# Sliding 8x8 windows of a 16x64x64x64 tensor: how the input loads are divided between the queues

## The chip, the cores and the metric

One core of one Trainium2 chip. The metric is the device time of one execution in microseconds (us); the program is a pure copy, so DMA and the copies inside the core's memory are all its work.

## The reference

```python
batch, c, h, w = (16, 64, 64, 64)      # x, float32; window_size 8, stride 4
n_h = (h - window_size) // stride + 1  # 15
n_w = (w - window_size) // stride + 1  # 15
for i in range(n_h):
    for j in range(n_w):
        result[:, i, j] = x[:, :, i*4 : i*4 + 8, j*4 : j*4 + 8]
```

The output has the shape (16, 15, 15, 64, 8, 8): 16.78 MB go in, 58.98 MB come out. Every input element is written up to four times.

## The kernel before

**Layout.** The whole input is held in the on-chip tile Lt (L is its view). A partition holds 32 channels of 16 rows of one image: the partition number is half * 64 + y * 32 + (image within y) * 4 + q. The half ch is the lower (0, channels 0 to 31, partitions 0 to 63) or the upper one (partitions 64 to 127), y one of two groups of eight images, q the quarter of the image's height. One channel of one partition is 16 rows x 64 columns, 4,096 bytes that lie together in memory.

**Loads.** Two kinds. The first FC = 8 channels of each half are *staged*: eight transfers (one for each q and half) bring them for all 16 images into the buffer GG, which the output does not need yet, at partitions 32 to 95. ScalarE issues the four of the lower half, SyncE the four of the upper one (L124). The other 24 channels go straight to Lt, by `load` (L61), which for a given half, y and q writes eight partitions, every fourth one. There are eight pairs (y, q), in order. For each of the first six (HWP = 6), SyncE loads channels 12 to 31 of the lower half (20 channels, 640 KB), GpSimd channels 8 to 11 of the lower half (SMALL = 4, 128 KB), and then channels 8 to 31 of the upper half (24 channels, 768 KB). For the last two pairs GpSimd loads 24 channels of both halves and SyncE nothing. So SyncE has 4 staging transfers and 6 loads, GpSimd 16 loads. Transfers of a kind share eight semaphores in turn: each one's issue waits until the one eight places before it has landed.

**Moves.** 16 copies (L141), two channels of 32 partitions each, take the staged channels from GG to Lt, y = 0 before y = 1. Every third is ScalarE's, the others VectorE's: six and ten.

**Output.** ScalarE and VectorE copy windows from Lt into tiles cut from GG (`part`, L192; `plain`, L212 and L150; `cross`, L225, L150 and L229; the last line, L256), and GpSimd writes each tile out by an indirect scatter (L158): one row of the tile for each partition, 16,384 bytes in `part` (index idx_y), 24,576 in the others (idx, idx_lo, idx_hi). A row whose index is made too large by FAR is dropped. In `cross`, every partition with q = 3 of one half is dropped: idx_lo drops those of partitions 0 to 63, idx_hi those of 64 to 127. There are six `part` tiles, five `plain` and ten `cross` ones, and two last tiles that SyncE stores (L257). The scatters come in this order: part, part, part, plain, part, plain, part, plain, part, plain, then cross tiles, lo and hi in turn, with one more plain in the middle. From the fourth tile on three buffers rotate, so a tile's copies wait until the scatter three tiles back has left its buffer. `part` tiles of y = 0 need only the loads of the first four pairs; `plain` tiles need all. All scatters stand in GpSimd's DMA queue behind its loads.

Of the kernel before, what the change touches and what calls it, by code (L numbers as in the profile page):

```python
# [10 lines left out]
def kernel(  # L11
# [7 lines left out]
    nc = tc.nc  # L19
    P = nc.NUM_PARTITIONS  # L20

    B, C, H, W = x.shape
# [8 lines left out]
    CH = 2  # L31
    HQ = P // (B * CH)
    CL = C // CH
    RB = H // HQ
# [5 lines left out]
    NY = B // YB  # L40
# [11 lines left out]
    L = Lt[:, :, 0 : RB * W].rearrange("p c (r w) -> p c r w", r=RB)  # L52
# [1 line left out]

    SMALL, HWP = 4, 6

    def load(eng, ch, y, q, c0, c1):
        p0 = ch * HP + y * QP + q  # L60
        eng.dma_start(out=L[p0 : p0 + QP - HQ + 1 : HQ, c0:c1, :, :], in_=x_v[ch, y, q, :, c0:c1, :])  # L61
# [11 lines left out]
    LF = 3 * CFREE // 2  # L73
# [38 lines left out]

    NG = 3
    TC = CFREE // (RB * W)
    FC = 8
    CP = RB * W + PAD
    GG = gpool.tile([P, NG * LF], f32)
    assert CH * FC * CP <= NG * LF
    S = [GG[:, ch * FC * CP : (ch + 1) * FC * CP].rearrange("p (c f) -> p c f", c=FC)[:, :, 0 : RB * W].rearrange("p c (r w) -> p c r w", r=RB) for ch in range(CH)]
    x_b = x.rearrange("b (ch cl) (hq r) w -> ch hq b cl (r w)", ch=CH, hq=HQ)  # L120
    for q in range(HQ):
        for ch in range(CH):
            s = S[ch][QP + q : QP + q + (B - 1) * HQ + 1 : HQ]
            (nc.scalar, nc.sync)[ch].dma_start(out=s, in_=x_b[ch, q, :, 0:FC, :])  # L124

    for y in range(NY):
        for q in range(HQ):
            hw = y * HQ + q < HWP
            if hw:
                load(nc.sync, 0, y, q, FC + SMALL, CL)  # L130
            load(nc.gpsimd, 0, y, q, FC, FC + SMALL if hw else CL)
            load(nc.gpsimd, 1, y, q, FC, CL)

    PC = TC // 2
    first = [(0, ch, c) for ch in range(CH) for c in range(0, FC, PC)]
    then = [(1, ch, c) for ch in range(CH) for c in range(0, FC, PC)]
    for n, (y, ch, c) in enumerate(first + then):
        f = slice(QP + y * QP, QP + (y + 1) * QP)
        d = slice(ch * HP + y * QP, ch * HP + (y + 1) * QP)
        copy = nc.vector.tensor_copy if n % 3 else nc.scalar.copy  # L140
        tc.keep_in_program_order(copy(out=L[d, c : c + PC, :, :], in_=S[ch][f, c : c + PC]))  # L141

    o_v = out.rearrange("b i j c r w -> (b i j) (c r w)")
    o_l = out.rearrange("b i j c r w -> (b i j c r w)").rearrange("(n f) -> n f", f=LF)
# [103 lines left out]
    for s in range(2):  # L248
        t = tile_()
        g = halves(t, 3)  # L250
        for n, ch, cols in line(NR - 1):
            for y in range(NY):
                d = slice(QP + y * QP, QP + (y + 1) * QP)
                f = slice(ch * HP + y * QP, ch * HP + (y + 1) * QP)
# [38 lines left out]
```

## Time and profile before

| | us |
|---|---|
| median of 3 runs (185.74 to 185.79) | 185.74 |
| the profiled execution | 185.73 |
| its span in the profile | 184.0 |
| VectorE busy | 142.8 |
| ScalarE busy | 141.6 |
| GpSimd busy | 39.5 |

The span is the time from the first to the last instruction of the profiled execution; 1.73 us of its time lie around it. Matrix work there is none. In the slices of the profile each digit is the busy share of one fortieth of the span, 4.6 us, in tenths; the DMA row is the mean over 16 DMA engines, and GB/s is what they moved. DMA queue q0 is GpSimd's, q1 SyncE's, q10 ScalarE's, q14 fetches instructions. "SPq" and "ACTq" rows are work of an engine's sequencer, such as issuing a transfer. In a timeline, the first number is the start and the second the time until the group's end, with the wait before it in brackets.

### The profile page before, as it was taken

How to read it: one execution, taken by the hardware profiler on the slowest of the kernel's cores; microseconds unless marked ns; L12 is line 12 of the kernel's file. 1: busy time of each engine (PE TensorE's matmuls, PEld its weight loads, DVE VectorE, ACT ScalarE, POOL GpSimd, SP SyncE). 2: the span in 40 equal slices, each digit the busy share in tenths (PEclk: the TensorE clock that was granted, in tenths of full speed). 3: DMA queues.
4: the chain of work that ended last, by engine and by line, in shares of the span. 5: the costliest groups of instructions: out<-in, count | busy, mean ns of one | idle time of the engine just before them, and what ended most of it. 6: DMA issues, size and time to landing. Idle time of an engine off the chain costs nothing.

```text
span 184.0 us, 501 instructions
## 1 busy us (share of the span) xinstructions
DVE 142.8 (78%) x183; ACT 141.6 (77%) x82; POOL 39.5 (21%) x42
## 2 busy tenths in 40 slices
DVE  4002999999999949979999599898798869978700
ACT  0002999999999969989899489889787869978700
POOL 7500763033330420230122202211220220220000
DMA  4999999999999999999999999999999999999993
GB/s 150 400 412 409 411 413 410 399 394 443 422 431 440 433 431 447 413 435 444 419 438 438 433 429 433 444 433 428 428 428 433 428 435 433 428 428 428 428 428 134
DMA packets 9828, 75.80 MB, mean 412 GB/s; under 512 B 3072, under 2 KB 3072, under 8 KB 7168
## 3 DMA queue, kind: packets, MB, share of 16 engines
q0 software_dynamic: 7504, 64.50, 83.2%
q1 hardware_dynamic: 1744, 9.18, 12.2%
q10 hardware_dynamic: 576, 2.10, 3.1%
q14 instruction: 4, 0.03, 0.0%
HBM read 16.78 MB, written 62.91 MB: 433 GB/s over the span
## 4 chain that ended last, share of the span: by engine, by line
DMA 68%; DVE 19%; issue 3%; POOL 2%; ACT 2%; ACTq 0%; DVEq 0%; PEldq 0%
DMA out_dram<-GG,idx_lo 26%; DMA out_dram<-GG,idx 21%; DMA Lt<-in_x_dram 14%; DVE GG L192 8%; DMA out_dram<-GG,idx_hi 8%; DVE GG L150 7%; POOL Lt L61 2%; ACT GG L256 2%; DVE GG L229 2%; DVE GG L212 1%; ACTq L288 0%; DVE GG L256 0%; DVEq L150 0%; POOL pi L77 0%; DVEq L212 0%
## 5 line engine op out<-in xcount | busy, mean ns | idle before, releaser
L225 ACT COPY GG<-Lt 64x2048 f32<-64x2048 f32 x30 | 56.9, 1897 | 9.6 <-DMA out_dram<-GG,idx 4.8
L150 DVE STREAM_SHUFFLE GG<-Lt 64x1024 f32<-64x1024 f32 (+1 forms) x35 | 50.6, 1444 | 0.9
L192 DVE COPY GG<-Lt 32x2048 f32<-32x2048 f32 x30 | 36.6, 1219 | 4.4 <-DMA out_dram<-GG,idx 3.4
L192 ACT COPY GG<-Lt 32x2048 f32<-32x2048 f32 x18 | 34.1, 1896 | 2.8 <-DMA out_dram<-GG,idx 2.4
L212 ACT COPY GG<-Lt 64x2048 f32<-64x2048 f32 x15 | 28.3, 1897 | 0.8 <-DMA out_dram<-GG,idx_lo 0.5
L141 DVE COPY Lt<-GG 32x2048 f32<-32x2048 f32 x10 | 11.9, 1236 | 13.8 <-DMA GG<-in_x_dram 13.7
L229 DVE COPY GG<-Lt 64x1024 f32<-64x1024 f32 x30 | 20.5, 683 | 0.6
L61 POOL DMA_DIRECT2D Lt<-in_x_dram x16 | 13.8, 873 | 17.5 <-DMA Lt<-in_x_dram 16.8
L158 POOL DMA_INDIRECT out_dram<-GG,idx_y x6 | 9.5, 1578 | 30.7 <-DVE GG L192 26.3
L141 ACT ACT_TABLE_LOAD x1 | 1.3, 1283 | 17.1 <-DMA GG<-in_x_dram 17.1
L212 DVE COPY GG<-Lt 64x2048 f32<-64x2048 f32 x10 | 12.1, 1221 | 0.3
L256 ACT COPY GG<-Lt 32x768 f32<-32x768 f32 x12 | 10.0, 830 | 1.8 <-DMA out_dram<-GG,idx_hi 1.2
L158 POOL DMA_INDIRECT out_dram<-GG,idx_lo x5 | 4.8, 963 | 30.1 <-DVE GG L229 30.1
L141 ACT COPY Lt<-GG 32x2048 f32<-32x2048 f32 x6 | 11.2, 1894 | 0.1
L256 DVE COPY GG<-Lt 32x1280 f32<-32x1280 f32 x12 | 9.8, 819 | 1.6 <-DMA out_dram<-GG,idx_hi 0.9
L158 POOL DMA_INDIRECT out_dram<-GG,idx x5 | 6.2, 1246 | 19.8 <-ACT GG L212 16.7
L158 POOL DMA_INDIRECT out_dram<-GG,idx_hi x5 | 4.9, 976 | 26.0 <-DVE GG L229 18.0
L150 DVE LOAD_MASK_SELECT GG<-Lt x35 | 0.3, 8 | 8.2 <-DMA out_dram<-GG,idx 3.7
L80 DVE TENSOR_SCALAR tb<-pi 128x1 int32<-128x1 int32 x1 | 0.2, 155 | 1.0 <-POOL pi L77 1.0
L83 DVE TENSOR_SCALAR tb<-tb 128x1 int32<-128x1 int32 x2 | 0.3, 153 | 0.0
L86 DVE TENSOR_TENSOR th<-tc,tq 128x1 int32<-128x1 int32 x2 | 0.3, 152 | 0.0
L77 POOL IOTA pi<- 128x1 int32 x1 | 0.1, 124 | 0.4 <-PEq L288 0.4
(20 smaller groups left out, 2.9 us busy)
## 6 DMA issues: line engine op xcount, KB each, us to landing
Lt<-in_x_dram POOLq DMA_DIRECT2D x10, 768.0 KB, 17.8
Lt<-in_x_dram SPq DMA_DIRECT2D x6, 640.0 KB
out_dram<-GG SPq DMA_DIRECT2D x2, 1536.0 KB, 10.1
GG<-in_x_dram ACTq DMA_DIRECT2D x4, 512.0 KB, 14.3
GG<-in_x_dram SPq DMA_DIRECT2D x4, 512.0 KB, 14.7
Lt<-in_x_dram POOLq DMA_DIRECT2D x6, 128.0 KB, 17.8
out_dram<-GG,idx_y POOLq DMA_INDIRECT x6, 12.1
out_dram<-GG,idx POOLq DMA_INDIRECT x5, 13.5
```

Of the source, the lines that this page charges most:

```text
L61: eng.dma_start(out=L[p0 : p0 + QP - HQ + 1 : HQ, c0:c1, :, :], in_=x_v[ch, y, q, :, c0:c1, :])
L80: nc.vector.tensor_scalar(out=d[:, :], in0=pi[:, :], scalar1=shift, scalar2=mask, op0=ALU.logical_shift_right, op1=ALU.bitwise_and)
L83: nc.vector.tensor_scalar(out=d[:, :], in0=a[:, :], scalar1=float(m), scalar2=None, op0=ALU.mult)
L86: nc.vector.tensor_tensor(out=d[:, :], in0=a[:, :], in1=b[:, :], op=op)
L141: tc.keep_in_program_order(copy(out=L[d, c : c + PC, :, :], in_=S[ch][f, c : c + PC]))
L150: nc.vector.stream_shuffle(out=out, in_=in_, mask=mask)
L158: st = nc.gpsimd.indirect_dma_start(out=rows, out_offset=bass.IndirectOffsetOnAxis(ap=ix[:, 0:1], axis=0), in_=g, in_offset=None, element_ ...
L192: (act if n % 3 == 0 else dve)(out=g[d * QP : (d + 1) * QP, ch], in_=L[f : f + QP, :, s * ST : s * ST + WS, cols],)
L212: (copy or (dve if m else shf))(out=g[d, n], in_=L[f, :, half * ST : half * ST + WS, cols])
L225: act(out=g[lo, n], in_=L[f, :, s * ST : s * ST + WS, cols])
L229: dve(out=g[hi, n, :, 0:ST], in_=L[f, :, (s + 1) * ST : RB, cols])
L256: copy(out=g[d, n, c0:c1], in_=L[f, c0:c1, s * ST : s * ST + WS, cols])
```

## The change

Four numbers change, and the loop with them. Seven channels of the upper half are staged in place of eight (FC = (8, 7)), so that SyncE's four staging transfers have 448 KB each and the upper half's loads 25 channels. SyncE loads the lower half's channels 10 to 31 (22 channels) in all eight pairs; in the first six pairs (SPLIT = 6) in two transfers, of 10 and of 12 channels, so there are 14. GpSimd loads in each pair two channels of the lower half (SMALL = 2, 64 KB) and 25 of the upper one (800 KB), 16 loads as before. Of the 16 moves two have one channel in place of two, one of VectorE's and one of ScalarE's; their order stays. Nothing of the output part changes.

```diff
-    SMALL, HWP = 4, 6
+    SMALL, SPLIT = 2, 6
...
-    FC = 8
+    FC = (8, 7)
...
-            (nc.scalar, nc.sync)[ch].dma_start(out=s, in_=x_b[ch, q, :, 0:FC, :])
+            (nc.scalar, nc.sync)[ch].dma_start(out=s, in_=x_b[ch, q, :, 0 : FC[ch], :])
 
     for y in range(NY):
         for q in range(HQ):
-            hw = y * HQ + q < HWP
-            if hw:
-                load(nc.sync, 0, y, q, FC + SMALL, CL)
-            load(nc.gpsimd, 0, y, q, FC, FC + SMALL if hw else CL)
-            load(nc.gpsimd, 1, y, q, FC, CL)
+            mid = (FC[0] + CL) // 2
+            for c0, c1 in [(FC[0] + SMALL, mid), (mid, CL)] if y * HQ + q < SPLIT else [(FC[0] + SMALL, CL)]:
+                load(nc.sync, 0, y, q, c0, c1)
+            load(nc.gpsimd, 0, y, q, FC[0], FC[0] + SMALL)
+            load(nc.gpsimd, 1, y, q, FC[1], CL)
 
     PC = TC // 2
-    first = [(0, ch, c) for ch in range(CH) for c in range(0, FC, PC)]
-    then = [(1, ch, c) for ch in range(CH) for c in range(0, FC, PC)]
-    for n, (y, ch, c) in enumerate(first + then):
+    moves = [(y, ch, c) for y in range(NY) for ch in range(CH) for c in range(0, FC[ch], PC)]
+    for n, (y, ch, c) in enumerate(moves):
+        e = min(c + PC, FC[ch])
...
-        tc.keep_in_program_order(copy(out=L[d, c : c + PC, :, :], in_=S[ch][f, c : c + PC]))
+        tc.keep_in_program_order(copy(out=L[d, c:e, :, :], in_=S[ch][f, c:e]))
```

More of the change, by code (lines that the diff above doesn't have):

```diff
@@ L114 @@
     TC = CFREE // (RB * W)
-    FC = 8
+    FC = (8, 7)
     CP = RB * W + PAD
     GG = gpool.tile([P, NG * LF], f32)
-    assert CH * FC * CP <= NG * LF
-    S = [GG[:, ch * FC * CP : (ch + 1) * FC * CP].rearrange("p (c f) -> p c f", c=FC)[:, :, 0 : RB * W].rearrange("p c (r w) -> p c r w", r=RB) for ch in range(CH)]
+    assert sum(FC) * CP <= NG * LF
+    S = [GG[:, ch * FC[0] * CP : (ch * FC[0] + FC[ch]) * CP].rearrange("p (c f) -> p c f", c=FC[ch])[:, :, 0 : RB * W].rearrange("p c (r w) -> p c r w", r=RB) for ch in range(CH)]
     x_b = x.rearrange("b (ch cl) (hq r) w -> ch hq b cl (r w)", ch=CH, hq=HQ)
```

## The prediction

> **What bounds the kernel now.** I read the page from its top: slices, DMA queues, chain of waits.
>
> ```profile
> span 184.0 us, 501 instructions
> DVE 142.8 (78%) x183; ACT 141.6 (77%) x82; POOL 39.5 (21%) x42
> DMA  4999999999999999999999999999999999999993
> GB/s 150 400 412 409 411 413 410 399 394 443 422 431 440 433 431 447 413 435 444 419 438 438 433 429 433 444 433 428 428 428 433 428 435 433 428 428 428 428 428 134
> DMA packets 9828, 75.80 MB, mean 412 GB/s; under 512 B 3072, under 2 KB 3072, under 8 KB 7168
> q0 software_dynamic: 7504, 64.50, 83.2%
> q1 hardware_dynamic: 1744, 9.18, 12.2%
> q10 hardware_dynamic: 576, 2.10, 3.1%
> q14 instruction: 4, 0.03, 0.0%
> DMA 68%; DVE 19%; issue 3%; POOL 2%; ACT 2%; ACTq 0%; DVEq 0%; PEldq 0%
> ```
>
> The DMA line is full from the second slice of 4.6 us to the last but one, while VectorE and ScalarE are idle for more than a fifth of the span, and 68% of the chain is DMA. So the 16 DMA engines are the bound, and there are two stages: nine slices of loads at about 410 GB/s, then stores at about 431. The loads end near 44.0 us: 0.69 MB in the first slice (4.6 us at 150 GB/s), the other 16.09 MB of the 16.78 MB input at some 408 GB/s, 39.4 us. The windows give the rates more closely, and the DMA view of 5 to 40 us gives the packets of the load stage:
>
> ```profile
> 5.00:40.00 35.00, 22.21 (x19) 22.63 (x13) 12.00 (x12) 1.00 1.03 407
> 10.00:15.00 5.00, 0.00 (x0) 0.00 (x0) 0.00 (x0) 1.00 1.04 413
> 60.00:100.00 40.00, 35.71 (x38) 36.50 (x21) 8.52 (x7) 1.00 1.00 432
> 100.00:160.00 60.00, 50.93 (x76) 50.79 (x27) 8.66 (x9) 1.00 1.01 432
> DMA packets 5414, 14.25 MB, mean 407 GB/s; under 512 B 1936, under 2 KB 1936, under 8 KB 5414
> ```
>
> The last number of a window is GB/s, the one before it the DMA share. The best load window, 413 GB/s, is one 4,096 B packet (one channel of one partition) in 16 x 4096 / 413,000 = 0.159 us on each engine. A store row of 24,576 B takes 16 x 24576 / 432,000 = 0.91 us on its engine, one of 16,384 B 0.607 us. A change of this kernel moves the end only if it changes the work of the engine that finishes last, or lets it run dry.
>
> **Which engines a load uses.** The packet counts tell. q1 is SyncE's queue: 4 staging transfers of 128 packets, 6 loads of 160 and 2 final stores of 64 make 1600 of its 1744. The 144 left over are completions: 16 each for the six 16-partition transfers (96), so 8 for each of the six loads. An 8-partition load from SyncE therefore runs on eight engines only. On q0 (GpSimd) the 16 loads are 2112 packets, the scatters 2528 written rows, and 37 transfers x 16 completions 592; of 7504 that leaves 2272 = 2112 + 160. The 160 are the rows that ten crossing scatters drop, and 2112 is one tiny packet for each load packet, which is what a load leaves if its data go to eight engines and as many empty entries to the other eight. Had GpSimd's big loads used SyncE's eight engines, the others would have idled and the rate been near half; spread over all 16, the other eight would have had 64 + 132 packets in place of 256 and run out 60 x 0.159 = 9.5 us early. Neither is in the slices. So GpSimd's loads, issued alternately for the lower and upper half, alternate between the eight engines: its small ones sit with SyncE's loads (set L), its 24-channel ones on the other eight (set H).
>
> Per engine, before: staging 64 packets for all; L 6 x (20 + 4) + 2 x 24 = 192; H 8 x 24 = 192. Both 256. Tiny entries: L 8 x 24 = 192, H 6 x 4 + 2 x 24 = 72. The price of a tiny one: 407 against 413 GB/s over 35 us is 0.51 us lost, with 1936 / 16 = 121 of them per engine, so 4 ns. The floor is zero.
>
> **Which set ends last.** Two of the last landings show it, in the timeline of the end:
>
> ```profile
> 149.85 0.96 POOL L158 DMA_INDIRECT out_dram<-GG,idx_hi  x1 [6.28 <-DVE GG L229]
> 157.21 0.96 POOL L158 DMA_INDIRECT out_dram<-GG,idx_lo  x1 [6.40 <-DVE GG L229]
> 163.18 5.10 ACT L256 COPY GG<-Lt 32x768 f32<-32x768 f32 x6 [1.18 <-DMA out_dram<-GG,idx_hi]
> 168.33 6.11 SPq L257 DMA_DIRECT2D out_dram<-GG  x2
> 168.68 5.10 ACT L256 COPY GG<-Lt 32x768 f32<-32x768 f32 x6 [0.40 <-DMA out_dram<-GG,idx_lo]
> ```
>
> ScalarE goes on when the idx_hi scatter issued at 149.85 has left its buffer, and again when the idx_lo scatter issued at 157.21 has: 168.68 - 163.18 = 5.50 us later. idx_lo drops every fourth row of partitions 0 to 63, so an engine reading those has 6 of 8 rows there, 6 x 0.91 = 5.46 us, while one reading partitions 64 to 127 has 8, 7.28 us. The interval is the six-row one. So the late engine reads the lower partitions, and the upper ones' engines were through the earlier scatter at least 7.28 - 5.50 = 1.8 us before it. At that point four idx_lo and four idx_hi scatters lie behind both sets, equal rows. The lag is real, and it lasts to the end.
>
> Is the lower-partition set L? The 120 additional tiny entries (0.5 us) make L late, which fits, but explains only part of 1.8 us. The Trainium skill's page "DMA: Bandwidth & Descriptors" states (section "Why a DMA increments its semaphore by 16 and not by 1") that the engine count divides the slowest dimension and that a hardware-generated transfer takes the lowest-numbered engines, and (section "The descriptor swizzle") that the first eight engines serve partitions 0 to 63. By that page L is the lower-partition set; the eight completions per SyncE load agree with its first half, no row here shows the second.
>
> **The change part by part.** Rows of the start:
>
> ```profile
> 0.74 3.09 SPq L124 DMA_DIRECT2D GG<-in_x_dram  x4
> 1.48 4.89 POOL L61 DMA_DIRECT2D Lt<-in_x_dram  x8 [0.52 <-issue]
> 4.82 13.21 SPq L61 DMA_DIRECT2D Lt<-in_x_dram  x6
> 17.17 11.99 DVE L141 COPY Lt<-GG 32x2048 f32<-32x2048 f32 x10 [13.72 <-DMA GG<-in_x_dram]
> 18.43 11.25 ACT L141 COPY Lt<-GG 32x2048 f32<-32x2048 f32 x6
> 29.50 18.61 DVE L192 COPY GG<-Lt 32x2048 f32<-32x2048 f32 x15 [0.35 <-DMA Lt<-in_x_dram]
> 36.57 1.75 POOL L158 DMA_INDIRECT out_dram<-GG,idx_y  x1 [4.38 <-DMA Lt<-in_x_dram]
> 47.00 5.62 ACT L212 COPY GG<-Lt 64x2048 f32<-64x2048 f32 x3
> 79.82 1.50 POOL L158 DMA_INDIRECT out_dram<-GG,idx  x1 [3.67 <-ACT GG L212]
> L61 SPq DMA_DIRECT2D Lt<-in_x_dram x6: 677/680/3817, 4.8 to 14.2; - x6
> ```
>
> *Packets.* The total stays 4096. Staging falls to 32 + 28 = 60 per engine. L gets 8 x (22 + 2) = 192, so 252: four fewer, -0.635 us. H gets 8 x 25 = 200, so 260: four more, +0.635 us. Tiny entries: L 8 x 25 = 200 (+8), H 8 x 2 = 16 (-56); eight more SyncE transfers leave eight more completions on L. At 4 ns: L -0.635 + 0.064 = **-0.57 us**, H +0.635 - 0.224 = +0.41 us. With free tiny entries L is -0.64 and H +0.64; at three times the price L is -0.44. H had 1.8 us of room, so L still ends last, 0.57 us earlier.
>
> *Staging moves.* One of VectorE's ten and one of ScalarE's six halve: 1.2 / 2 and 1.88 / 2 us off moves that end at 17.17 + 11.99 = 29.16 and 18.43 + 11.25 = 29.68. What is late next is the load that VectorE waits for until 29.50, so at most 0.4 us is gained there, off the path: the first scatter is issued by 36.57 + 1.75 = 38.3, and its queue is busy with loads until about 44. I count nothing.
>
> *SyncE's issues.* Eight more at the median 0.68 us are 5.4 us; from its ninth load on each waits for the load eight before it. Queued behind are only the two final stores at 168.33. Nothing; GpSimd issues 16 loads as before, smaller and larger in turn.
>
> *Do the stores follow?* If loads end 0.57 us earlier, stores must be ready as much earlier. The tightest early one is the eighth scatter, issued by 79.82 + 1.50 = 81.32. Loads to 44.0, then five scatters of 128 x 16,384 B (4.86 us each) and two of 128 x 24,576 B (7.28) make 82.9: 1.6 us of lead, 1.0 after the change, and H, which would be dry first, comes 0.41 us later. Still covered.
>
> *A rule against it.* The Trainium skill's page "DMA: Bandwidth & Descriptors" (section "Rules for kernel authors") says that small transfers should be joined and that those under 64 KB are mostly overhead; its fit is about 2 us fixed per transfer, so eight more in series would by an estimate from it be 16 us. In the window 10 to 15 us, with 128 KB transfers in flight, the queues still moved 413 GB/s, so that cost was covered.
>
> Sum: 185.73 us for the profiled execution (its span 184.0 and 1.73 around it; the median is 185.74) less 0.57: **185.2 us**.
>
> **Rivals.** *No gain.* Of the 1.8 us lag the tiny entries explain 0.5. If the other 1.3 comes from something that recurs at a fixed place (the four instruction fetches of q14 have to be served by some engine), the last engine may be delayed anew: 185.7. For it: the unexplained part. Against: the engines never idle, so less work stays less work. Chance 0.20.
>
> *The sets are the other way round.* If SyncE's loads sit on the engines of partitions 64 to 127, the late ones are H, and get +0.41 (up to +0.64): 186.1, half within, half beyond the bound. Chance 0.07.
>
> *Slower, by queue order.* An engine of L alternates between SyncE's entries and GpSimd's. After the change it has 32 + 6 x 24 + 2 x 23 = 222 of the one and 8 x 29 = 232 of the other, GpSimd starting later (1.48 against 0.74): SyncE's should run out first, with ten or more of GpSimd's left, nearly all tiny. Were GpSimd's out first, the first scatter's 0.607 us rows would slip in between SyncE's last loads, one for one. It begins at about five packets left, where the load lands at 47.0, the time of the first copy that needs it (ScalarE at 47.00), and costs time from about seven, when the 1.0 us of lead is gone. With ten left: 44.0 + 6.1 = 50.1, copies 3.1 us late, 2.1 us of it beyond the lead: 185.2 + 2.1 = 187.3. Before, two whole GpSimd pairs stood behind, so the trace has no such case. Chance 0.10.
>
> *Cost per transfer.* If all of the 0.51 us lost in 5 to 40 us were a cost per transfer (about 22 loads), eight more would be 0.19 us: 185.4, within the bound. This is the rule above as rows allow it. Chance 0.03.
>
> **How the numbers follow.** 0.2% is 0.37 us, about what a measurement of this kernel can tell from no change. Forecast 0.60, faster. Same: 0.20 + 0.03 + half of 0.07 = 0.27. Slower: 0.10 + half of 0.07 = 0.13. The range is 184.7 (0.64 us with free tiny entries, and 0.4 more should the late engine lose part of its unexplained 1.3) to 186.2 (the swapped sets); outside are the queue-order case and some hundredths at each end.
>
> **What would show it.** Right: 2,192 packets on q1 (448 staging, 1,408 load and 128 store packets, 96 + 14 x 8 completions: still eight engines per load), small packets on q0 fewer by 384, load slices nearer 413 GB/s, the interval between the last idx_hi and idx_lo landings still near 5.5 us, both about 0.5 us earlier. Wrong: a slice under 390 GB/s after 44 us (a dry engine), a wait of ScalarE or VectorE on an input load after 47 us (queue order), or an interval of 7.3 us at the end (the other set late).

## The result and the profile after

| | median, us | ratio to before (95% interval) |
|---|---|---|
| before | 185.74 | |
| changed | 185.07 (184.96 to 185.17) | 0.9963 (0.9952 to 0.9975) |
| changed, measured again beside the last experiments | 185.00 (before: 185.69) | 0.9971 (0.9961 to 0.9981) |

The changed kernel is faster by 0.3 to 0.4%, 0.54 to 0.69 us; 185.2 was forecast. The profiled execution took 184.96 us against 185.73. Its page, the lines that answer to those of before:

```profile
span 183.2 us, 516 instructions
DMA  4999999999999999999999999999999999999994
GB/s 154 397 413 410 410 410 411 411 412 437 426 440 456 429 395 440 438 429 433 429 453 429 429 431 429 429 435 429 429 429 435 429 431 419 429 429 435 429 429 182
DMA packets 9509, 75.80 MB, mean 414 GB/s; under 512 B 2753, under 2 KB 2753, under 8 KB 6849
q0 software_dynamic: 6736, 62.92, 81.1%
q1 hardware_dynamic: 2192, 10.75, 14.3%
q10 hardware_dynamic: 576, 2.10, 3.1%
DMA 75%; DVE 11%; POOL 3%; ACT 2%; issue 2%; ACTq 0%; DVEq 0%; PEldq 0%
```

The DMA row is as full as before, and the bytes are the same. The eighth and ninth slices, the last of pure loading, went from 399 and 394 GB/s to 411 and 412; the experiments show that this is not the gain. The last slice has 182 GB/s in place of 134: the engines now end closer together. q1 has the 2,192 packets forecast, so SyncE's shorter loads still run on eight engines; q0 lost 768 packets, 384 of data and 384 tiny ones.

The start and the end of the timeline:

```profile
29.17 17.27 ACT L196 COPY GG<-Lt 32x2048 f32<-32x2048 f32 x9 [0.52 <-DMA Lt<-in_x_dram]
36.27 1.74 POOL L162 DMA_INDIRECT out_dram<-GG,idx_y  x1 [5.64 <-DVE GG L196]
46.46 5.62 ACT L216 COPY GG<-Lt 64x2048 f32<-64x2048 f32 x3
...
156.63 0.96 POOL L162 DMA_INDIRECT out_dram<-GG,idx_lo  x1 [5.64 <-DVE GG L233]
162.40 5.11 ACT L260 COPY GG<-Lt 32x768 f32<-32x768 f32 x6 [0.62 <-DMA out_dram<-GG,idx_hi]
168.79 5.10 ACT L260 COPY GG<-Lt 32x768 f32<-32x768 f32 x6 [1.29 <-DMA out_dram<-GG,idx_lo]
```

The first scatter is issued 0.3 us earlier, and no copy waits for an input load at 46.46: the queue-order rival did not come about. The idx_hi landing for which the last copies wait, a point where both sets have the same rows behind them, is at 162.40 in place of 163.18: set L, which is last there, gained 0.78 us. The idx_lo landing follows after 6.39 us, neither the 5.46 us of six rows nor the 7.28 us of eight. It is now H's: H has eight rows there, so it was at the even point at 168.79 - 7.28 = 161.5. Before, the same reading bounded H by 168.68 - 7.28 = 161.4. **L's end moved by 0.78 us and H's by hardly anything.** L's lag behind H went from 1.8 us or more to 0.9.

The trace also records when a transfer lands on each of the 16 engines, and these records refine the reading. Before, that idx_hi scatter lands on eight engines at 160.99 to 161.25 us (H), on seven at 161.78 to 162.14 and on the last one at 163.10: of the 1.8 us, about 1 us is one engine alone. In the idx_lo scatter the seven, with their six rows, land at 167.36 to 167.72 before and at 166.79 to 167.32 in the changed kernel, 0.53 us earlier in the mean, where 0.57 was forecast. The one last engine lands at 162.32 in place of 163.10, 0.78 us earlier.

### The profile page after: what moved, and what is told of

It is laid out like the page before. It is cut to its first block, busy times and chain, and to the rows that moved or that the text cites. A ratio compares the mean times of both kernels' runs of the same rounds, so it can differ in the third digit from the quotient of the medians.

```text
span 183.2 us, 516 instructions
## 1 busy us (share of the span) xinstructions
DVE 142.1 (78%) x183; ACT 140.8 (77%) x82; POOL 40.0 (22%) x42
## 3 DMA queue, kind: packets, MB, share of 16 engines
q1 hardware_dynamic: 2192, 10.75, 14.3%
## 4 chain that ended last, share of the span: by engine, by line
DMA 75%; DVE 11%; POOL 3%; ACT 2%; issue 2%; ACTq 0%; DVEq 0%; PEldq 0%
DMA out_dram<-GG,idx 28%; DMA out_dram<-GG,idx_lo 21%; DMA Lt<-in_x_dram 20%; DVE GG L154 7%; DMA out_dram<-GG,idx_hi 6%; POOL Lt L61 3%; ACT GG L260 2%; DVE GG L233 2%; DVE GG L196 2%; DVE GG L216 1%; ACTq L292 0%; DVEq L154 0%; POOL pi L77 0%; DVEq L216 0%; PEldq L292 0%
## 5 line engine op out<-in xcount | busy, mean ns | idle before, releaser
L145 DVE COPY Lt<-GG 32x2048 f32<-32x2048 f32 (+1 forms) x10 | 11.3, 1172 | 13.6 <-DMA GG<-in_x_dram 13.5
L145 ACT COPY Lt<-GG 32x2048 f32<-32x2048 f32 (+1 forms) x6 | 10.3, 1752 | 0.1
```

The lines of the kernel that those rows point to most:

```text
L145: tc.keep_in_program_order(copy(out=L[d, c:e, :, :], in_=S[ch][f, c:e]))
```

## The experiments

Theory: the end is set by the work of the eight engines of set L, which hold SyncE's loads; only packets taken from them count. Rivals: SyncE's queue is the better place for loads; or shorter staging lets the rest begin earlier. Ratios are to the kernel before on the same chip.

### The two halves of the change apart

`sync_only`:

```diff
-    FC = (8, 7)
+    FC = (8, 8)
```

> The change without its staging part: FC = (8, 8), SyncE's 22 channels in all eight pairs in 14 transfers. Per engine set L (SyncE's eight engines) keeps 64 + 8 x 24 = 256 load packets and H keeps 256. Theory (the end is set by the packets of L): L as before, plus eight completions, so 185.7 to 185.8 us, no change; H alone gets quicker by its 56 tiny entries (0.2 us). Rival 'SyncE's queue is the gain' (fewer loads through GpSimd, 448 fewer tiny entries): most of the gain is here, 185.1 to 185.3. Rival 'shorter staging is the gain': 185.7.

`stage_only` (the loop of before with FC = (8, 7)):

```diff
-    SMALL, SPLIT = 2, 6
+    SMALL, HWP = 4, 6
...
+            hw = y * HQ + q < HWP
+            if hw:
+                load(nc.sync, 0, y, q, FC[0] + SMALL, CL)
+            load(nc.gpsimd, 0, y, q, FC[0], FC[0] + SMALL if hw else CL)
```

> The change's staging part alone: seven channels of the upper half staged, 25 loaded by GpSimd; SyncE loads 20 channels in six pairs as before. L 60 + 192 = 252 packets, H 60 + 200 = 260; tiny entries L 200, H 72. Theory: L -0.6 us, H +0.63 against at least 1.8 us of room before, so 185.1 to 185.3 (H may come within reach: before, an engine of H was 1.8 us ahead at a point of equal rows; now about 0.6). Rival 'SyncE's queue is the gain': 185.7.

Measured: `sync_only` 185.72 us, 1.0006 (0.9997 to 1.0015), no change; `stage_only` 184.94 us, 0.9962 (0.9948 to 0.9975), the whole gain. SyncE's part does nothing by itself. The end of the timeline of `sync_only`, then of `stage_only`:

```profile
163.17 5.10 ACT L260 COPY GG<-Lt 32x768 f32<-32x768 f32 x6 [1.19 <-DMA out_dram<-GG,idx_hi]
168.60 5.10 ACT L260 COPY GG<-Lt 32x768 f32<-32x768 f32 x6 [0.34 <-DMA out_dram<-GG,idx_lo]
```

```profile
162.56 5.10 ACT L260 COPY GG<-Lt 32x768 f32<-32x768 f32 x6
169.53 5.10 ACT L260 COPY GG<-Lt 32x768 f32<-32x768 f32 x6 [1.87 <-DMA out_dram<-GG,idx_lo]
```

In `sync_only` the idx_hi landing stands where it stood before (163.18) and the interval is the six-row one, 5.43 us: L is last, with its 256 packets. In `stage_only` the copies after idx_hi no longer wait for it (no bracket), and H, back-reckoned, is at 169.53 - 7.28 = 162.25, against 161.5 in the changed kernel, where it has the same packets and 56 tiny entries fewer: a first sign that a tiny entry costs more than 4 ns, though not all of the difference is theirs. L's seven engines, with the same packets in both kernels, also land later in `stage_only` (idx_lo at 167.31 to 167.68), only 0.1 us ahead of before in the mean; what moved by the forecast size in its trace is the last engine, from 163.10 to 162.47. The slices of the two, `sync_only` first, show that a higher rate in the load stage is not the gain:

```profile
GB/s 161 389 417 408 408 413 410 411 410 428 442 428 440 428 426 438 424 454 428 420 458 428 433 429 428 428 428 433 428 428 428 428 429 428 428 428 428 428 428 134
```

```profile
GB/s 144 392 414 411 410 412 412 393 398 436 427 433 450 434 409 434 440 425 442 420 440 429 434 436 429 429 440 429 434 424 424 429 431 424 424 434 429 429 429 225
```

`sync_only` has 411 and 410 GB/s in the eighth and ninth slices and no gain; `stage_only` keeps 393 and 398 and has all of it. The last slice, 134 and 225, shows how close together the engines end, and not the gain either: `stage_only_8_5` below has 235 there and gains nothing. A mean over 16 engines says nothing of the one that ends last.

### The mirror

`stage_7_8`:

```diff
-    FC = (8, 7)
+    FC = (7, 8)
```

> The change mirrored: seven channels of the lower half staged, eight of the upper, FC = (7, 8). As many bytes staged and as many moves as in the change, SyncE 23 channels per pair. L 60 + 8 x 25 = 260 packets, H 60 + 192 = 252. Theory: L +0.64 us, so 186.3 to 186.5, slower than before. Rivals 'shorter staging' and 'SyncE's queue': as the change or better, 185.0 to 185.1.

Measured: 186.15 us, 1.0028 (1.0017 to 1.0039), slower by 0.3 to 0.7 us. As much staging is saved as in the change and SyncE carries more, so both rivals fall; L has four packets more in place of four fewer, and the sign turns. Its end:

```profile
163.70 5.10 ACT L260 COPY GG<-Lt 32x768 f32<-32x768 f32 x6 [1.19 <-DMA out_dram<-GG,idx_hi]
169.14 5.10 ACT L260 COPY GG<-Lt 32x768 f32<-32x768 f32 x6 [0.34 <-DMA out_dram<-GG,idx_lo]
```

Again 5.44 us, six rows: the set that got SyncE's additional packets is the one that reads partitions 0 to 63 and ends last. This is the link that the prediction could not show from rows, and it agrees with what the Trainium skill's page "DMA: Bandwidth & Descriptors" (section "The descriptor swizzle") says, for a transfer to 128 partitions, of the first eight engines.

### How far the balance can be pushed

`stage_8_6` and `stage_8_5`:

```diff
-    FC = (8, 7)
+    FC = (8, 6)
```

```diff
-    FC = (8, 7)
+    FC = (8, 5)
```

> The change with six channels of the upper half staged, FC = (8, 6). L 56 + 192 = 248 packets, H 56 + 208 = 264. In the changed kernel H's last engine was 0.9 us ahead of L's last at a point of equal rows (162.4 against 168.8 - 7.3 = 161.5). Theory: L another 0.6 us less, H 0.6 more, so H is last by about 0.3: 184.8 us, at the balance. Rival 'shorter staging is the gain': again as much as the first channel brought, 184.4. Rival 'SyncE's queue is the gain': 185.1, as changed.

> The change with five channels of the upper half staged, FC = (8, 5): L 52 + 192 = 244 load packets, H 52 + 216 = 268, 16 tiny entries on H. Theory: H is now last, four packets (0.64 us) beyond stage_8_6, where the two sets were about level: 185.3 to 185.5 us, the gain half given back. Rival 'shorter staging is the gain': at or below 184.8.

Measured: `stage_8_6` 184.84 us, 0.9959 (0.9945 to 0.9972); `stage_8_5` 185.09 us, 0.9974 (0.9963 to 0.9984). The second channel brings at most a little, the third brings nothing more. A gain by shorter staging would have gone on growing.

### The price of a tiny entry

`stage_only_8_5` is `stage_only` with FC = (8, 5): the same load packets on both sets as `stage_8_5`, but 72 tiny entries on H in place of 16.

> The same packets as stage_8_5 (L 244, H 268) with the division of before: SyncE 20 channels in six pairs, GpSimd the rest. H, which is last, gets 72 tiny entries in place of 16. Theory with 4 ns for a tiny entry: 0.22 us over stage_8_5, 185.5 to 185.7. If they are free: as stage_8_5. At three times the price: 0.67 us over it.

Measured: 185.73 us, 1.0008 (0.9999 to 1.0017), where `stage_8_5` has 0.9974: 0.34%, 0.63 us, for 56 entries on each engine of H, 11 ns each if all of it is theirs. End of `stage_8_5`, then of `stage_only_8_5`:

```profile
162.47 5.11 ACT L260 COPY GG<-Lt 32x768 f32<-32x768 f32 x6 [0.18 <-DMA out_dram<-GG,idx_hi]
169.29 5.11 ACT L260 COPY GG<-Lt 32x768 f32<-32x768 f32 x6 [1.72 <-DMA out_dram<-GG,idx_lo]
```

```profile
163.30 5.10 ACT L260 COPY GG<-Lt 32x768 f32<-32x768 f32 x6
170.25 5.10 ACT L260 COPY GG<-Lt 32x768 f32<-32x768 f32 x6 [1.85 <-DMA out_dram<-GG,idx_lo]
```

In both the wait for idx_lo is the long one: H is last and arrives 0.96 us later in the second. But the two kernels also differ in which queue loads the last two pairs, and L, with the same packets and tiny entries in both, comes later as well. At the landing of the last input load the means are 43.20 and 43.47 us for L, 45.39 and 46.15 for H: H lost 0.49 us more than L, 9 ns for each entry.

Other records agree with about that. The trace has each packet's own duration: 9 ns for a 4-byte entry, 159 in the median for a 4,096-byte packet. And in the last two pairs before the change, an engine that holds the data of one GpSimd load has 24 tiny entries and a completion of the next one behind them: the next load lands there 0.17 to 0.20 us (means of eight engines) after the first, 7 to 8 ns for each. **A tiny entry costs 7 to 9 ns**, about twice the 4 of the prediction.

### Which engines GpSimd's loads take

`upper_first`:

```diff
-            load(nc.gpsimd, 0, y, q, FC[0], FC[0] + SMALL)
             load(nc.gpsimd, 1, y, q, FC[1], CL)
+            load(nc.gpsimd, 0, y, q, FC[0], FC[0] + SMALL)
```

> The changed kernel with GpSimd's two loads of a pair issued in the other order, the upper half's 25 channels first. Theory (GpSimd's 8-partition loads alternate between the eight engines, whatever they hold): the big ones now fall on SyncE's eight engines, L 60 + 8 x (22 + 25) = 436 packets, H 76. L then works 184 packets x 0.159 = 29 us longer: about 214 us, with a load rate near half once staging is through. Rival 'GpSimd's loads spread over all engines, or over the free ones': 185.

Measured: 215.53 us in its one timed run. Swapping two lines that do not depend on each other costs 30 us. Its slices:

```profile
span 213.8 us, 517 instructions
GB/s 188 321 294 211 222 210 222 222 222 210 331 379 407 310 220 294 451 397 405 353 417 434 412 449 437 402 423 442 437 437 419 423 437 429 437 428 405 432 428 189
```

From the fourth slice to the tenth, 5.3 us each, 210 to 222 GB/s is moved: half of the load rate of about 410, so eight engines of 16. GpSimd's 8-partition loads take the two sets in turn; which set a load gets is decided by its place in the order of issue, not by the partitions it writes.

### The halves of SyncE's loads

`no_split` and `no_split_again` (SPLIT = 0), `no_split_8_6` (SPLIT = 0 and FC = (8, 6)), beside `after_again`, the changed kernel, and `stage_8_6_again`:

> The changed kernel with SPLIT = 0: SyncE's 22 channels in one transfer per pair, 8 in place of 14. Theory: as the changed kernel, 185.0 to 185.1 (six completions fewer on L). Rival 'each transfer has a price of its own': 6 x 0.02 = 0.1 us quicker. Rival 'the halves make the load land in time': slower.

> The changed kernel once more, on one chip with the next three, so that they can be set against it: 0.996 of before.

> SPLIT = 0 beside the changed kernel. Theory (neither set's packets differ): the same as it within 0.1 us. Rival 'the halves bring something': 0.2 to 0.3 us slower, as the last comparison read.

> FC = (8, 6) beside the changed kernel. Theory with 11 ns for a tiny entry, the price that stage_8_5 and stage_only_8_5 gave: L -0.54 us against the change, H +0.64; the change left L's last engine about 0.3 us behind H's at the end, so the two cross: 0.1 to 0.3 us quicker than the change. Rival 'shorter staging': 0.5 us quicker.

> FC = (8, 6) and SPLIT = 0: the candidate with the fewest transfers at the balance. Theory: as stage_8_6, within 0.1 us. Rival 'the halves bring something': 0.2 to 0.3 us slower than stage_8_6.

Measured: `no_split` 185.26 us, 0.9980 (0.9971 to 0.9989), which looked worse than the change; beside it on one chip `no_split_again` 185.16 us, 0.9973 (0.9963 to 0.9982) against `after_again` 0.9971 (0.9961 to 0.9981): no difference. `stage_8_6_again` 184.93 us, 0.9960 (0.9946 to 0.9974), and `no_split_8_6` 185.10 us, 0.9971 (0.9961 to 0.9981). None of these can be told from another; whether FC = (8, 6) beats the change by the 0.1 to 0.2 us of its medians stays open.

## Why the prediction was right

**The frame.** DMA engines busy throughout, two sets of eight, the end set by the set with SyncE's loads: each part has a run of its own. Eight engines to a load: the half rate of `upper_first`, and 8 completions for each of 14 SyncE loads. L last: `stage_7_8` and the six-row intervals. Four packets off L as the whole gain: `stage_only` against `sync_only`. SyncE's added issues cost nothing that a run shows (`sync_only`, `no_split_again`); the shorter moves and the new waits were not tried alone.

**The mis-sized term** is the price of a tiny entry: 4 ns in the prediction, 7 to 9 by the traces. The working compared the mean load rate (407 GB/s) with the best load window (413), but that window already had 188 small packets in it, so the difference showed only part of their cost. With 9 ns, L changes by -0.635 + 16 x 0.009 = -0.49 us, and H by +0.635 - 56 x 0.009 = +0.13 in place of +0.41. L's seven engines moved by -0.53. The error did not reach the forecast because it was small on L (16 entries) and large on H (56), and H did not decide.

**The lag of 1.8 us** was read rightly, but it is not one of a whole set, and the tiny entries account for little more than the prediction said. Where the last input load lands, before the change, L is 0.62 us behind H in the mean, against 0.5 counted for the 120 additional entries (at 7 to 9 ns each they would make 0.8 to 1.1). Most of the rest is the one engine. It falls behind where q14 fetches instructions (8,192 bytes and 0.31 us each time in the trace). Before, the last engine is 0.05 us behind the next at the landing at 143.1; a fetch starts at 148.35; at the landing at 150.4 it is 1.09 behind. `sync_only` has 0.03, a fetch at 147.43 and 1.26; the changed kernel 0.14, a fetch at 148.48 and 1.08. No run moves a fetch, so that it causes the delay, more than three times its own length, is not shown. So the guess behind the "no gain" rival (chance 0.20) pointed at the right place; the delay came again in the changed kernel, but on top of the shorter work of L, and did not undo the gain. That the last engine gained 0.78 us where the seven gained 0.53 was not forecast and has no part in the working; that the measured 0.54 to 0.69 us lies on the 0.57 so closely is partly luck.

**The wrong marker.** The prediction expected the idx_hi to idx_lo interval to stay near 5.5 us. It took H's 1.8 us of room as enough for that. But in the idx_lo scatter H has two rows more, 1.82 us, so H is last there as soon as L's lag falls below 1.82 us, which any gain on L brings about. The interval should have been forecast above 5.5 us; the 6.39 us measured is a sign of the gain, not against it. For the same reason only the idx_hi landing came earlier: the idx_lo one, also forecast about 0.5 us earlier, is at 168.79 against 168.68, since H is last there.

With 9 ns, and H 1.8 us ahead before, the later of the two sets gives for each run, against its measured change (ratio less one, times the median of before beside it):

| run | L, us | H less 1.8, us | later of the two | measured |
|---|---|---|---|---|
| `sync_only` | +0.07 | -2.3 | +0.1 | +0.1 |
| `stage_only` | -0.56 | -1.2 | -0.6 | -0.7 |
| changed | -0.49 | -1.7 | -0.5 | -0.7, -0.5 |
| `stage_8_6` | -1.0 | -1.0 | -1.0 | -0.8, -0.7 |
| `stage_8_5` | -1.6 | -0.4 | -0.4 | -0.5 |
| `stage_only_8_5` | -1.7 | +0.1 | +0.1 | +0.1 |
| `stage_7_8` | +0.7 | -2.9 | +0.7 | +0.5 |

The table fits the times. It does not fit every set by itself: in `sync_only` H should land 0.5 us earlier than before, and its eight engines land at 160.87 to 161.10 in place of 160.99 to 161.25. `stage_8_6` gained somewhat less than the table says. Its end:

```profile
161.98 5.10 ACT L260 COPY GG<-Lt 32x768 f32<-32x768 f32 x6 [0.23 <-DMA out_dram<-GG,idx_hi]
168.73 5.10 ACT L260 COPY GG<-Lt 32x768 f32<-32x768 f32 x6 [1.65 <-DMA out_dram<-GG,idx_lo]
```

L is at 161.98, 0.42 us better than in the change, and H at 168.73 - 7.28 = 161.45, no later than there (161.5), where the packets would have it 0.64 later. But `stage_8_6_again` and `no_split_8_6` have L at 162.50 and 162.64, no better than `after_again` (162.29) and `no_split_again` (162.53): the second channel does not move L in the traces. Its packets do show while the loads run: L lands the last input load at 43.76 to 44.16, 0.9 us ahead of H (44.74 to 44.97). In the stores this lead is lost: at idx_hi all but one of the 16 engines land between 161.13 and 161.67. It is not lost by waiting for stores. Counted over all 16 engines, the packet records leave 0.5 us without a packet between 45 and 180 us, against 7.5 in `stage_7_8` and 5.7 in `stage_only_8_5`, where one set is 2 us or more ahead at the last load and does run dry. What takes the lead in `stage_8_6` stays open.

The rivals: queue order did not occur (no copy waits for a load at 46.46), but no run provoked it; the swapped sets are refuted by `stage_7_8`; a cost per transfer by `no_split_again`, whose six fewer transfers change nothing.

## What to carry to other kernels

When all DMA engines look busy, ask which of them ends last: count packets per engine and not per queue, since a transfer over few partitions uses few engines, and move packets off the late set; which queue issues them is beside the point. A landing that alternates between two patterns of dropped rows is a clock for each set, and reading it at a point where both have done the same work shows the room left; where the trace has the landings of the single engines, they tell a late set from one late engine. A price taken from the difference between a mean and a best window is a lower bound if the best window pays it too.

## What the runs showed of the hardware that I had not expected

A load over eight partitions from GpSimd's queue leaves a 4-byte entry on the other eight engines for each packet of data (2,112 for 2,112 in the kernel before). Each costs its engine 7 to 9 ns by the traces, about 5% of a 4,096-byte packet's 159 ns; before the change, L's 192 of them come to 1.3 to 1.7 us. After an instruction fetch of 0.31 us one engine was about 1 us behind the others (0.05 to 1.09 us before the change, fetch at 148.35), and the end waited for it. And the order of two independent loads on one queue decided 30 us (`upper_first`).
